# Joining the third product chain of a 512-token decoder's feed-forward units: one wide PSUM bank, read by a copy and additions

## The chip, the cores and the metric

The kernel runs on one core of a Trainium2 chip. Its time is the device time of one execution in microseconds (us); a lower time is better. The engines that matter here are TensorE (PE in the profile, with PEld for its weight loads), VectorE (DVE), ScalarE (ACT) and GpSimd (POOL, which here only issues transfers). Each takes its instructions in the order in which the program lists them, and waits at an instruction until what it needs is there. PSUM is the memory that TensorE writes its sums to; it is cut into banks of 512 float32 values for each of 128 partitions, and ScalarE and VectorE read it.

## The reference

A decoder trunk of two layers works on 512 tokens of 1024 channels. Each layer has a token mixer (a recurrent one in layer 0, a Conformer convolution in layer 1), a cross-attention into 256 memory tokens, and a gated feed-forward part. The change touches the feed-forward part alone:

```
def conv_ffn(x, norm, w_up, dw_w, dw_b, w_down):
    h = rms_norm(x, norm) @ w_up                      # 1024 -> 2 * 3072
    g = causal_dwconv(h[..., :D_FF], dw_w, dw_b)      # 3 taps along the tokens
    u = h[..., D_FF:]
    return (jax.nn.gelu(g) * u) @ w_down              # 3072 -> 1024
```

All numbers are float32. Products are made at more than one-pass precision: each operand is split into a high part (`hi`) and a low rest (`lo`), and `hi*hi + hi*lo + lo*hi` is summed.

## The kernel before, in words

The feed-forward part of a layer is worked in 24 *units*, one for each 128 hidden channels of the gate `g` and of the values `u`. Units 0 and 1 are plain; units 2 to 23 use a scheme of Strassen's kind with seven products of half size. A product multiplies one 512-by-128 block of weights (four chunks of 128 rows: `a11`, `a12`, `a22`, `s1` to `s4`) with one half-size operand made of the tokens (`T1` to `T4`, `B11`, `B21`, `B22`), for 256 tokens. Function `m` issues one product, by way of `Seven.product`. The sums of the products go to three *chains*, each a PSUM tile: `G` (products a11 and a12), `F` (a copy of a11, then s2, s3 and a22) and `H` (s1 and s4).

In a *narrow* product each chunk takes three matmuls over 256 columns (lines L187, L188, L189 of the helper `mm3`): `hi` weights on the high half of the operand, `hi` weights on its low half, `lo` weights on its high half. In a *joined* product the operand's high and low halves lie side by side, so that each chunk takes two matmuls (line L817): `hi` weights on all 512 columns, and `lo` weights on the first 256. The chain's bank then holds two halves that have to be added when it is read; `gather` does that with a ScalarE copy of the right half (L955) and a VectorE addition (L172, the line of the helper `add`). Units 6 to 21 (`WIDE`) have joined passes in `G` and `F`; `H` is narrow in all units. In these units `H` lies in the one bank of pool `stat` (`bufs=1`), so each unit takes the same bank again.

The order of every engine's work is written out by hand (`manual_schedule`). One unit `c`, in TensorE's order: s1 into `H`, s2 into `F`, a12 into `G`, s3 into `F`, 24 matmuls of the down projection into two `aux` banks, a11 of the next unit (`ahead`), s4 into `H`, a22 into `F`. `H` is read twice: after s3, for the right half of `f`, and at the unit's end, in `gating`, for the right half of `g`. `gating` is a generator: its first step stands at the end of its own unit, the others are woven into the next unit by `next(left, None)`.

Lines that the text speaks of, in a unit's order, beginning with the first step of `gating`: L172 addition of `H` to `g`; L961 `g` times the norm (VectorE); L939 first tap (ScalarE); L955 and L172 gather of `f`; L969 `f` times the norm; L942 two taps; L955 and L172 gather of `u` after s2; L899 two ScalarE copies that seed the `aux` banks; L944 GELU; L859 and L866 the high and low parts of a block of weights (ScalarE, then VectorE); L976 product of `f` and the gate; L979 and L981 its high and low parts; L201 and L204 the same of the down projection's weights; L904 two copies of the `aux` banks back to x; L992 the copy of the next unit's a11 chain into `F`.

Five lines that set the buffers:

```
    tmp = ctx.enter_context(tc.tile_pool(name="tmp", bufs=8))
    psum = ctx.enter_context(tc.tile_pool(name="ps", bufs=5, space=bass.MemoryType.PSUM))
    stat = ctx.enter_context(tc.tile_pool(name="stat", bufs=1, space=bass.MemoryType.PSUM))
    aux = ctx.enter_context(tc.tile_pool(name="aux", bufs=2, space=bass.MemoryType.PSUM))
    big = ctx.enter_context(tc.tile_pool(name="big", bufs=15))
```

Of the kernel before, what the change touches and what calls it, by code (L numbers as in the profile page):

```python
# [12 lines left out]
AF = mybir.ActivationFunctionType  # L13
# [8 lines left out]
M = 256  # L22
# [40 lines left out]
def trunk(ctx: ExitStack, tc: tile.TileContext, I: dict, out: list):  # L63
    nc = tc.nc
    V, A, G, PE = nc.vector, nc.scalar, nc.gpsimd, nc.tensor
# [14 lines left out]
    def nm(s):  # L80
        uid[0] += 1
        return f"{s}_{uid[0]}"

    def act_r():
        return act.tile([P, T], F32R, tag="act", name=nm("act"))
# [10 lines left out]
    def tmp_f(n=T):  # L96
        return tmp.tile([P, n], F32, tag="tmp", name=nm("tmp"))

    def main_ps():
        return psum.tile([P, T], F32, tag="mm", name=nm("mm"))  # L100
# [4 lines left out]
    wide = [True, 0]  # L105
# [6 lines left out]
    def stat_ps():  # L112
        return stat.tile([P, T], F32, tag="stat", name=nm("stat"))
# [57 lines left out]
    def add(out, a, b):  # L171
        V.tensor_tensor(out, a, b, op=ALU.add)  # L172
        return out
# [705 lines left out]
    def ffn(layer, norm, nxt, seven, pairs):  # L879
# [37 lines left out]
        def high(c, name):  # L917
            if c in pairs and (c, name) not in done:
                pairs[c].high(name)

        def low(c, name):
            if c in pairs and (c, name) not in done:
                pairs[c].low(name)
                done.add((c, name))

        def both(c, name):
            high(c, name)
            low(c, name)

        def times_r(out, ps, at):  # L930
            V.tensor_tensor(out[:, at], ps, norm.r[:, at], op=ALU.mult)

        left_half, right_half = slice(0, M), slice(M, T)

        def gate_conv(c, g):

            y = tmp_f()
            dw = lambda j: col("f_dw_w", (layer * 3 + j) * CF + c)
            A.activation(y, g, AF.Identity, scale=dw(2), bias=col("f_dw_b", layer * CF + c))  # L939
            yield y  # L940
            for s in (1, 2):
                V.scalar_tensor_tensor(y[:, s:], g[:, : T - s], dw(2 - s), y[:, s:], op0=ALU.mult, op1=ALU.add)  # L942
            yield y
            A.activation(y, y, AF.Gelu_apprx_tanh)  # L944
            yield y

        def wide(c):
            return c in WIDE
# [4 lines left out]
        def gather(out, ps):  # L953

            A.activation(out, ps[:, M:], AF.Copy)  # L955
            add(out, ps[:, :M], out)

        def gating(c, g, f, u, F, H):
            add(g[:, right_half], H, u[:, :M])
            if wide(c):  # L960
                V.tensor_tensor(g, g, norm.r, op=ALU.mult)  # L961
            else:
                V.tensor_tensor(g[:, right_half], g[:, right_half], norm.r[:, right_half], op=ALU.mult)
            conv = gate_conv(c, g)
            y = next(conv)
            yield
            if wide(c):
                gather(f[:, left_half], F)
                V.tensor_tensor(f, f, norm.r, op=ALU.mult)  # L969
            else:  # L970
                times_r(f, F, left_half)
            next(conv)
            yield
            next(conv)
            yield
            V.scalar_tensor_tensor(y, f, -1.0, y, op0=ALU.mult, op1=ALU.mult)  # L976
            yield
            ys[c] = act_r(), act_r()
            A.activation(ys[c][0], y, AF.Copy)  # L979
            yield  # L980
            V.tensor_tensor(ys[c][1], y, ys[c][0].bitcast(F32), op=ALU.subtract)  # L981

        def m(c, ps, block, j, first=True):
            seven.product(ps, pairs[c].w[block], j, first)

        def ahead(c):

            G, F = bank(c), bank(c)
            m(c, G, "a11", seven.B11)
            if c == WIDE[0] + 1:  # L990
                PE.matmul(F, pairs[c].w["a11"][0][:, :P], seven.both(seven.B11, 0), start=True, stop=True)
            A.activation(F, G, AF.Copy)  # L992
            return G, F

        def unit(c):

            nonlocal left, chains
            G, F = chains
            down, seeded = downs.get(c), c > GC
            H = (stat_ps if wide(c) else main_ps)()[:, :M]  # L1000
            m(c, H, "s1", seven.T1)
            if c <= second:
                high(c + 1, "s3")
            next(left, None)
            if c <= second:
                low(c + 1, "s3")

            m(c, F, "s2", seven.T2, False)
            u, f, g = tmp_f(), tmp_f(), tmp_f()
            if wide(c):  # L1010
                gather(u[:, :M], F)
            else:
                A.activation(u[:, :M], F, AF.Copy)
            if c == first:
                both(c + 2, "a11")
            if down:
                d = [down.bank(i, seeded) for i in range(2)]
            next(left, None)
            both(c + 1, "s3")
            next(left, None)  # L1020
            high(c + 1, "a22")

            m(c, G, "a12", seven.B21, False)
            next(left, None)
            next(left, None)
            high(c, "s4")
            if c == second:
                high(c + 2, "a11")
            low(c, "s4")
            if wide(c):  # L1030
                gather(g[:, left_half], G)
            elif c > second:
                times_r(g, G, left_half)

            m(c, F, "s3", seven.T3, False)
            if wide(c):
                gather(u[:, M:], F)
            else:
                A.activation(u[:, M:], F, AF.Copy)
            add(f[:, right_half], H, u[:, M:])  # L1040
            if c <= second:
                times_r(g, G, left_half)
            if c == second:
                low(c + 2, "a11")
            low(c + 1, "a22")
            if not wide(c):
                V.tensor_tensor(f[:, right_half], f[:, right_half], norm.r[:, right_half], op=ALU.mult)
            both(c + 2, "a11")
            high(c + 1, "a12")
            low(c + 1, "a12")  # L1050
            if c == WIDE[0] - 2:
                seven.put_aside()
            elif c == WIDE[0] - 1:
                seven.put_beside(seven.B21)
            if down:
                for ks in (range(GC - 1), (GC - 1,)):
                    for i in range(2):
                        down.products(i, d[i], seeded, ks)
            if c + 3 in pairs:
                pairs[c + 3].load()  # L1060
            if c + 2 in pairs and c > first:
                pairs[c + 2].load_second()
            if c > second and c + 1 in downs:
                downs[c + 1].w.high()
                downs[c + 1].w.low()
            if c + 2 in downs and first < c <= CF - 2:
                downs[c + 2].load()
            high(c + 1, "s1")
            low(c + 1, "s1")
            high(c + 1, "s2")  # L1070
            low(c + 1, "s2")
            if c == second:
                downs[c + 1].w.high()
                downs[c + 1].w.low()
            if down:
                down.home(0, d[0], seeded)

            if c + 1 in pairs:
                chains = ahead(c + 1)
            if down:  # L1080
                down.home(1, d[1], seeded)
            if c == WIDE[0] - 2:
                seven.put_beside(seven.B11)

            m(c, H, "s4", seven.B22, False)
            m(c, F, "a22", seven.T4, False)
            if c == WIDE[0] - 1:
                seven.put_beside(seven.B22)
            left = gating(c, g, f, u, F, H)
            next(left)  # L1090

# [87 lines left out]
        with tc.manual_schedule(engines=ORDERED):  # L1179
            opening()  # L1180
            for c in range(PLAIN, CF):
                unit(c)
            for _ in left:
                pass
# [801 lines left out]
```

## Time and profile before

| | before |
|---|---|
| time, median of 3 runs (lowest to highest) | 1423.07 us (1421.4 to 1423.74) |
| the profiled execution: its own time | 1425.19 us |
| the profiled execution: span of its trace | 1423.3 us |
| granted TensorE clock, mean | 0.998 |
| TensorE busy in the span | 1411.7 us |
| VectorE busy | 1115.4 us |
| ScalarE busy | 934.0 us |
| units 6 to 21 of layer 0 in the trace | 430.57 us to about 676 us |
| units 6 to 21 of layer 1 in the trace | 1114.81 us to about 1360 us |

The span is the stretch from the first to the last record of the trace. A row of the timeline has the start of a piece of work in us from the span's start, its length in us, the engine, the line, the operation, what it writes and reads, the shape, and how many instructions follow each other; in brackets stands the idle time before it and the instruction whose end it waited for. Two instructions of an engine that don't depend on each other overlap by their pipelines' length, so the next starts before the one before has ended.

### The profile page before, as it was taken

Reading aid. Unit: us, or ns where it says so; the run is one execution under the profiler, and the core shown is the slowest. Engines: PE = TensorE matmul, PEld = TensorE weight load, DVE = VectorE, ACT = ScalarE, POOL = GpSimd, SP = SyncE. Lnnn points to the kernel's source line nnn. Section 1 sums busy time; section 2 is a strip of 40 time slices with the busy share of each in tenths; the row PEclk is TensorE's granted clock in tenths of the full one; section 3 lists DMA queues with packets and bytes.
Section 4 is the critical chain, followed back from the end, with each engine's and each line's share of the span. In section 5 each row is a group of like instructions: output and inputs, shape, how many; then the busy total and the mean of one; then the engine's idle time right before and its main releaser. Section 6 shows DMA issues by size and latency. Waiting matters only on the chain.

```text
span 1423.3 us, 21777 instructions
## 1 busy us (share of the span) xinstructions
PE 1411.7 (99%) x8012; PEld 1228.0 (86%) x8012; DVE 1115.4 (78%) x1860; ACT 934.0 (66%) x1688; POOL 316.9 (22%) x333
## 2 busy tenths in 40 slices
PE   9999999999999999999999999999999999999998
PEld 7988888998898888888988777899889888888897
DVE  6987776778877777777789997968788777777775
ACT  7578744776577666666666547766756766666664
POOL 0001310110122222222008993011002222222211
PEclk9999999999999999999999999999999999999999
DMA  8523232544387777777433454345438777777741
GB/s 302 195 78 100 94 118 82 113 118 133 97 205 167 172 172 172 169 173 169 134 104 119 119 158 153 105 89 130 116 96 195 176 175 166 176 173 168 174 122 60
DMA packets 80027, 204.26 MB, mean 144 GB/s; under 512 B 9008, under 2 KB 9520, under 8 KB 79920
## 3 DMA queue, kind: packets, MB, share of 16 engines
q1 hardware_dynamic: 50832, 150.15, 32.4%
q0 software_dynamic: 28800, 52.44, 21.5%
q8 instruction: 63, 1.03, 0.3%
q14 instruction: 44, 0.36, 0.1%
q10 hardware_dynamic: 288, 0.27, 0.1%
HBM read 145.16 MB, written 2.10 MB: 103 GB/s over the span
## 4 chain that ended last, share of the span: by engine, by line
PE 86%; DVE 3%; issue 3%; DMA 3%; POOL 2%; ACT 2%; SPq 0%; POOLq 0%; ACTq 0%; DVEq 0%
PE mm L817 16%; PE mm L187 13%; PE mm L188 13%; PE mm L189 13%; PE aux L187 7%; PE aux L188 7%; PE aux L189 7%; PE stat L187 2%; PE stat L189 2%; PE stat L188 2%; PE mm L465 2%; DMA raw<-in_wv 1%; DVE wlo L168 1%; DMA raw<-wa 1%; ACT whi L167 1%
## 5 line engine op out<-in xcount | busy, mean ns | idle before, releaser
L187 PE MATMUL mm<-act,whi 128*128 128x512 f32 (+2 forms) x805 | 296.5, 370 | 0.9 <-ACT act L979 0.9
L188 PE MATMUL mm<-act,whi 128*128 128x512 f32 (+2 forms) x805 | 296.8, 369 | 0.6 <-DVE act L182 0.5
L189 PE MATMUL mm<-act,wlo 128*128 128x512 f32 (+2 forms) x805 | 296.5, 368 | 0.0
L187 PEld LDWEIGHTS mm<-act,whi 128*128 128x128 f32 x805 | 151.5, 188 | 27.2 <-ACT act L979 1.6
L188 PEld LDWEIGHTS mm<-act,whi 128*128 128x128 f32 x805 | 151.7, 188 | 26.5 <-DVE act L168 1.0
L189 PEld LDWEIGHTS mm<-act,wlo 128*128 128x128 f32 x805 | 151.7, 188 | 25.0 <-DVE wlo L168 0.6
L866 DVE TENSOR_TENSOR bigr<-raw,bigr 128x512 fp32r<-128x512 f32 x176 | 120.8, 687 | 61.0 <-ACT bigr L859 57.3
L187 PE MATMUL aux<-act,whi 128*128 128x512 f32 x399 | 155.6, 390 | 0.0
L188 PE MATMUL aux<-act,whi 128*128 128x512 f32 x399 | 155.5, 390 | 0.0
L189 PE MATMUL aux<-act,wlo 128*128 128x512 f32 x399 | 155.2, 389 | 0.0
L859 ACT ACTIVATE bigr<-raw 128x512 fp32r<-128x512 f32 x176 | 109.4, 623 | 69.8 <-DVE wlo L204 66.2
L872 POOL DMA_DIRECT2D raw<-wa x100 | 87.4, 893 | 299.7 <-DVE bigr L866 195.9
L167 ACT ACTIVATE whi<-raw 128x1024 fp32r<-128x1024 f32 (+1 forms) x95 | 96.4, 1020 | 86.6 <-PE mm L188 43.3
L817 PE MATMUL mm<-bigr,bigr 128*128 128x512 f32 (+1 forms) x768 | 150.6, 338 | 0.0
L817 PEld LDWEIGHTS mm<-bigr,bigr 128*128 128x128 f32 x768 | 118.3, 189 | 14.3
L869 POOL DMA_DIRECT2D raw<-raw x50 | 43.2, 865 | 371.7 <-DVE wlo L866 285.1
L172 DVE TENSOR_TENSOR tmp<-mm,tmp 128x256 f32<-128x256 f32 x194 | 77.8, 417 | 40.4 <-ACT tmp L955 37.9
L168 DVE TENSOR_TENSOR wlo<-raw,whi 128x1024 fp32r<-128x1024 f32 (+1 forms) x75 | 90.2, 1209 | 19.7 <-ACT whi L167 19.0
L817 PE MATMUL mm<-act,whi 128*128 128x512 f32 x256 | 95.5, 396 | 0.0
L189 PEld LDWEIGHTS aux<-act,wlo 128*128 128x128 f32 x399 | 74.9, 188 | 15.9
L188 PEld LDWEIGHTS aux<-act,whi 128*128 128x128 f32 x399 | 75.0, 188 | 15.5
L187 PEld LDWEIGHTS aux<-act,whi 128*128 128x128 f32 x399 | 75.0, 188 | 14.3
(378 smaller groups left out, 3504.9 us busy)
## 6 DMA issues: line engine op xcount, KB each, us to landing
raw<-wa POOLq DMA_DIRECT2D x150, 256.0 KB, 3.4
wa<-in_wpair SPq DMA_DIRECT2D x88, 256.0 KB, 3.8
raw<-in_wpair SPq DMA_DIRECT2D x44, 512.0 KB, 3.7
big<-in_wdown SPq DMA_DIRECT2D x42, 512.0 KB, 4.6
raw<-raw POOLq DMA_DIRECT2D x50, 256.0 KB, 4.0
raw<-in_pw SPq DMA_DIRECT2D x24, 512.0 KB, 3.3
raw<-in_win SPq DMA_DIRECT2D x20, 512.0 KB, 3.3
raw<-in_wk SPq DMA_DIRECT2D x16, 512.0 KB, 3.3
```

Source lines behind the costliest of these rows:

```text
L167: A.activation(hi, src, AF.Copy)
L168: fetched[1] = (eng or V).tensor_tensor(lo, src, hi.bitcast(F32), op=ALU.subtract)
L172: V.tensor_tensor(out, a, b, op=ALU.add)
L187: PE.matmul(ps, wh, xh, start=first, stop=False, skip_group_check=onto)
L188: PE.matmul(ps, wh, xl, start=False, stop=False, skip_group_check=onto)
L189: return PE.matmul(ps, wl, xh, start=False, stop=last, skip_group_check=onto)
L465: PE.matmul(p, m[j], x, start=k == 0 and j == 0 and x is hi, stop=k == C - 1 and x is lo)
L817: PE.matmul(to, part, by, start=first and c == 0 and i == 0, stop=c == 3 and i == 1, skip_group_check=True)
L859: A.activation(self.w[name][0], self.block(name), AF.Copy)
L866: V.tensor_tensor(lo, self.block(name), hi.bitcast(F32), op=ALU.subtract)
L869: G.dma_start(self.r, self.z, accum_op=ALU.add)
L872: G.dma_start(block, self.a22, accum_op=ALU.add)
```

## The change

In units 6 to 21 the chain `H` is joined too. Its tile is now the whole bank of 512 columns, and s1 and s4 take the form of two matmuls for each chunk, as in `G` and `F`. The bank's two halves are read so: for `f`, by two VectorE additions straight from the bank, one after the other; for `g`, by a ScalarE copy of the right half into a new tile `low_part` of pool `tmp`, an addition of the left half, and an addition of `low_part`.

```
         def gating(c, g, f, u, F, H):
-            add(g[:, right_half], H, u[:, :M])
             if wide(c):
+                low_part = tmp_f(M)
+                A.activation(low_part, H[:, M:], AF.Copy)
+            add(g[:, right_half], H[:, :M], u[:, :M])
+            if wide(c):
+                add(g[:, right_half], low_part, g[:, right_half])
                 V.tensor_tensor(g, g, norm.r, op=ALU.mult)
...
         def unit(c):
...
-            H = (stat_ps if wide(c) else main_ps)()[:, :M]
+            H = stat_ps() if wide(c) else main_ps()[:, :M]
             m(c, H, "s1", seven.T1)
...
-            add(f[:, right_half], H, u[:, M:])
+            add(f[:, right_half], H[:, :M], u[:, M:])
+            if wide(c):
+                add(f[:, right_half], H[:, M:], f[:, right_half])
```

On TensorE each of the products s1 and s4 goes from 12 matmuls of 256 columns to 4 of 512 and 4 of 256, in the same place. On the other engines the order shows what follows, for unit 8 of layer 0 (all units from 6 to 21 are alike). The names are those of the program with a running number; the numbers differ between the two programs.

ScalarE at the unit's end, before: the high part of block s2 of the next unit (L859), the two copies of the down projection's banks to x with the copy of a11 between them, the first tap, and the gathers of `f` and `u`. `waits` names the engines or transfer queues that the instruction has to wait for.

```order
L859 ACTIVATE bigr_4840<-raw_4504 128x512 [waits DMASW2_49,DVE_49]
L904 ACTIVATE x<-aux_4752 128x512 [waits PE_49]
L992 ACTIVATE mm_4846<-mm_4845 128x512 [waits PE_49]
L904 ACTIVATE x<-aux_4754 128x512
L939 ACTIVATE tmp_4879<-tmp_4749,par 128x512 [waits DVE_49]
L955 ACTIVATE tmp_4748<-mm_4686 128x256 [waits PE_49]
L955 ACTIVATE tmp_4907<-mm_4846 128x256 [waits PE_49]
```

The same place after the change (line numbers behind the edit are higher by 4 or 6):

```order
L859 ACTIVATE bigr_4829<-raw_4501 128x512 [waits DMASW2_49,DVE_49]
L904 ACTIVATE x<-aux_4740 128x512 [waits PE_49]
L996 ACTIVATE mm_4835<-mm_4834 128x512 [waits PE_49]
L904 ACTIVATE x<-aux_4742 128x512
L961 ACTIVATE tmp_4862<-stat_4713 128x256 [waits PE_49]
L939 ACTIVATE tmp_4867<-tmp_4737,par 128x512 [waits DVE_49]
L955 ACTIVATE tmp_4736<-mm_4679 128x256 [waits PE_49]
```

The copy of the bank's right half (L961) is a new row, behind the second L904 and ahead of the first tap.

VectorE in the unit's middle, before: the gather of `g`, the gather of `u` after s3, the addition of `H` to `f`, and the low parts of three blocks and of the down projection's weights.

```order
L172 TENSOR_TENSOR tmp_4749<-mm_4685,tmp_4749 128x256 [waits Activation_49]
L172 TENSOR_TENSOR tmp_4747<-mm_4686,tmp_4747 128x256 [waits Activation_49]
L172 TENSOR_TENSOR tmp_4748<-stat_4721,tmp_4747 128x256 [waits DVE_49]
L866 TENSOR_TENSOR bigr_4763<-wa_4667,bigr_4763 128x512 [waits DMAHW5_49]
L866 TENSOR_TENSOR wlo_4795<-raw_4665,whi_4794 128x512 [waits DMAHW0_49,Activation_49]
```

And after:

```order
L172 TENSOR_TENSOR tmp_4737<-mm_4678,tmp_4737 128x256 [waits Activation_49]
L172 TENSOR_TENSOR tmp_4735<-mm_4679,tmp_4735 128x256 [waits Activation_49]
L172 TENSOR_TENSOR tmp_4736<-stat_4713,tmp_4735 128x256 [waits DVE_49]
L172 TENSOR_TENSOR tmp_4736<-stat_4713,tmp_4736 128x256 [waits DVE_49]
L866 TENSOR_TENSOR bigr_4751<-wa_4660,bigr_4751 128x512 [waits DMAHW5_49]
L866 TENSOR_TENSOR wlo_4784<-raw_4658,whi_4783 128x512 [waits DMAHW0_49,Activation_49]
```

One addition from the bank follows the other, and it reads what the first has written.

VectorE at the unit's end, before: the low parts of s1 and s2 of the next unit, the addition of `H` to `g`, the multiplication by the norm, and the gather of `f`.

```order
L866 TENSOR_TENSOR bigr_4837<-raw_4504,bigr_4837 128x512 [waits DMASW1_49,Activation_49]
L866 TENSOR_TENSOR bigr_4840<-raw_4504,bigr_4840 128x512 [waits DMASW2_49,Activation_49]
L172 TENSOR_TENSOR tmp_4749<-stat_4721,tmp_4747 128x256 [waits PE_49]
L961 TENSOR_TENSOR tmp_4749<-tmp_4749,r_3614 128x512 [waits DVE_49]
L172 TENSOR_TENSOR tmp_4748<-mm_4686,tmp_4748 128x256 [waits Activation_49]
L969 TENSOR_TENSOR tmp_4748<-tmp_4748,r_3614 128x512 [waits DVE_49]
```

And after:

```order
L866 TENSOR_TENSOR bigr_4826<-raw_4501,bigr_4826 128x512 [waits DMASW1_49,Activation_49]
L866 TENSOR_TENSOR bigr_4829<-raw_4501,bigr_4829 128x512 [waits DMASW2_49,Activation_49]
L172 TENSOR_TENSOR tmp_4737<-stat_4713,tmp_4735 128x256 [waits Activation_49]
L172 TENSOR_TENSOR tmp_4737<-tmp_4862,tmp_4737 128x256 [waits DVE_49]
L965 TENSOR_TENSOR tmp_4737<-tmp_4737,r_3614 128x512 [waits DVE_49]
L172 TENSOR_TENSOR tmp_4736<-mm_4679,tmp_4736 128x256 [waits Activation_49]
L973 TENSOR_TENSOR tmp_4736<-tmp_4736,r_3614 128x512 [waits DVE_49]
```

The first addition from the bank, which waited for TensorE, now waits for ScalarE; a second addition, of the copied half, stands between it and the multiplication.

## The prediction

> **What bounds the kernel now.** I read the busy shares first, then one wide unit of layer 0 by stretches, then the timeline of that unit engine by engine, and last the table of waits over all wide units of the layer.
>
> ```profile
> PE 1411.7 (99%) x8012; PEld 1228.0 (86%) x8012; DVE 1115.4 (78%) x1860; ACT 934.0 (66%) x1688; POOL 316.9 (22%) x333
> 507.59:522.95 15.36, 15.36 (x90) 13.53 (x89) 11.80 (x20) 10.39 (x21) 3.45 (x5) 1.00 0.72 173
> ACT bigr L859 <- DVE wlo L204: 27.8, 15, 1.9
> 506.17 1.58 PE L817 MATMUL mm<-bigr,bigr 128*128 128x512 f32 x8
> 507.59 0.28 PE L187 MATMUL stat<-bigr,bigr 128*128 128x256 f32 x1
> 509.02 1.56 PE L817 MATMUL mm<-bigr,bigr 128*128 128x512 f32 x8
> 510.43 0.40 PE L817 MATMUL mm<-act,whi 128*128 128x512 f32 x1
> 511.83 1.58 PE L817 MATMUL mm<-bigr,bigr 128*128 128x512 f32 x8
> 520.11 0.28 PE L187 MATMUL stat<-act,bigr 128*128 128x256 f32 x1
> 521.53 0.75 PE L817 MATMUL mm<-bigr,bigr 128*128 128x512 f32 x3
> ```
>
> TensorE is the bound: in the unit from one s1 (507.59) to the next (522.95) it is busy for all of 15.36 us at full granted clock (1.00). VectorE works 11.80 us of that and ScalarE 10.39 us, so both look as if they had room. The question is where their idle time lies, and for that their rows stand here in time order, over a unit and into the next.
>
> ```profile
> 506.42 0.42 DVE L172 TENSOR_TENSOR tmp<-stat,tmp 128x256 f32<-128x256 f32 x1
> 506.87 0.69 DVE L961 TENSOR_TENSOR tmp<-tmp,r 128x512 f32<-128x512 f32 x1
> 508.71 0.42 DVE L172 TENSOR_TENSOR tmp<-mm,tmp 128x256 f32<-128x256 f32 x1 [1.15 <-ACT tmp L955]
> 509.17 0.69 DVE L969 TENSOR_TENSOR tmp<-tmp,r 128x512 f32<-128x512 f32 x1
> 509.78 1.53 DVE L942 SCALAR_TENSOR_TENSOR tmp<-tmp,par,tmp 128x511 f32<-128x511 f32 x2
> 511.23 0.42 DVE L172 TENSOR_TENSOR tmp<-mm,tmp 128x256 f32<-128x256 f32 x1
> 513.12 0.69 DVE L866 TENSOR_TENSOR bigr<-raw,bigr 128x512 fp32r<-128x512 f32 x1 [1.47 <-ACT bigr L859]
> 513.73 0.69 DVE L976 SCALAR_TENSOR_TENSOR tmp<-tmp,tmp 128x512 f32<-128x512 f32 x1
> 515.11 0.69 DVE L981 TENSOR_TENSOR act<-tmp,act 128x512 fp32r<-128x512 f32 x1 [0.70 <-ACT act L979]
> ...
> 517.10 0.42 DVE L172 TENSOR_TENSOR tmp<-stat,tmp 128x256 f32<-128x256 f32 x1
> 517.44 0.68 DVE L866 TENSOR_TENSOR bigr<-wa,bigr 128x512 fp32r<-128x512 f32 x1
> ...
> 519.24 1.22 DVE L204 TENSOR_TENSOR wlo<-big,whi 128x1024 fp32r<-128x1024 f32 x1
> 520.38 1.47 DVE L866 TENSOR_TENSOR bigr<-raw,bigr 128x512 fp32r<-128x512 f32 x2
> 521.77 0.42 DVE L172 TENSOR_TENSOR tmp<-stat,tmp 128x256 f32<-128x256 f32 x1
> 522.22 0.69 DVE L961 TENSOR_TENSOR tmp<-tmp,r 128x512 f32<-128x512 f32 x1
> ```
>
> ```profile
> 507.60 0.82 ACT L939 ACTIVATE tmp<-tmp,par 128x512 f32<-128x512 f32 x1 [0.33 <-DVE tmp L961]
> 508.32 0.36 ACT L955 ACTIVATE tmp<-mm 128x256 f32<-128x256 f32 x1
> 510.63 0.38 ACT L955 ACTIVATE tmp<-mm 128x256 f32<-128x256 f32 x1 [1.95 <-PE mm L817]
> 511.95 0.62 ACT L944 ACTIVATE tmp<-tmp 128x512 f32<-128x512 f32 x1
> 512.47 0.62 ACT L859 ACTIVATE bigr<-raw 128x512 fp32r<-128x512 f32 x1
> 514.45 0.63 ACT L979 ACTIVATE act<-tmp 128x512 fp32r<-128x512 f32 x1 [0.84 <-DVE tmp L976]
> 520.49 0.63 ACT L859 ACTIVATE bigr<-raw 128x512 fp32r<-128x512 f32 x1 [1.85 <-DVE wlo L204]
> 521.03 0.58 ACT L904 ACTIVATE x<-aux 128x512 f32<-128x512 f32 x1
> 521.51 0.59 ACT L992 ACTIVATE mm<-mm 128x512 f32<-128x512 f32 x1
> 522.03 0.59 ACT L904 ACTIVATE x<-aux 128x512 f32<-128x512 f32 x1
> ```
>
> These idle times are not room: VectorE and ScalarE hand work to each other all around the unit. From L961 at 506.87, each step starts within 0.05 us of the end of its input, or as soon as its engine takes the next instruction: L961, L939, gather of `f` (L955, L172), L969, L942; L944, L859, L866 (513.12), L976, L979, L981, low parts up to L204; its end (519.24 + 1.22 = 520.46) lets ScalarE make the high part of s2 (520.49; the table shows the same wait in 15 units), whose low part is the second L866 of the row at 520.38, and then L172 (521.77) and L961 again (522.22). This **loop** of two engines takes 522.22 - 506.87 = 15.35 us, like TensorE, with one slack: L942 ends at 509.78 + 1.53 = 511.31, but L944 starts only at 511.95 (its engine waited 1.95 us for TensorE ahead of it). So the loop's own length is 15.35 - (511.95 - 511.34) = 14.74 us, 0.61 us below the period.
>
> **The change part by part.** *TensorE.* A joined product takes 1.40 to 1.42 us from its start to that of the next (506.17 to 507.59, 509.02 to 510.43, 510.43 to 511.83), a narrow one 1.43 (507.59 to 509.02) and 1.42 (520.11 to 521.53). Against a joined mean of 1.41 that saves 0.02 and 0.01 us; bounds are 0 and 0.05. In 32 wide units it is 1.0 us, with TensorE alone at 15.33 us a unit. No weight load or transfer is added, and SP's and POOL's issues keep their places.
>
> *Second addition for `f`.* Behind 517.10 stands a dependent addition. A dependent step after such an addition comes 0.45 us later (506.42 to 506.87), an independent one 0.34 (517.10 to 517.44); here the second addition waits for the first, then L866 follows it at 0.34, so the step after is later by 0.45. All steps from L866 to L204 and to ScalarE's 520.49 move with it: **+0.45 us** in the loop.
>
> *Copy of `H`'s right half.* It stands behind the second L904, and the first addition to `g` now waits for ScalarE, not for TensorE. The trace has no such copy; the nearest row is the gather's copy of the same shape from PSUM, 0.36 to 0.38 us, and I take 0.37. From ScalarE's 520.49: L904 +0.54, L992 +0.48, L904 +0.52, the copy +0.48 (the step from 521.03 to 521.51), its length 0.37, hand-over 0.03: 2.42 us to the addition. Before, it started 521.77 - 520.49 = 1.28 us after. That is **+1.14 us**. Bounds: 1.10 with a copy of 0.36 and no hand-over, and 1.35 if the copy took the 0.58 us of a copy of double width (521.03).
>
> *Second addition for `g`.* It reads SBUF; a row of two SBUF operands of this shape has the same 0.42:
>
> ```profile
> L764 DVE TENSOR_TENSOR tmp<-tmp,tmp 128x256 f32<-128x256 f32 x16 | 6.7, 419 | 0.7 <-ACT tmp L758 0.7
> ```
>
> It depends on the first addition, and L961 on it: **+0.45 us** (bound below: 0.34, the step of an independent one).
>
> *The new loop* is 14.74 + 0.45 + 1.14 + 0.45 = 16.78 us, over TensorE's 15.33. Each period grows by 16.78 - 15.35 = 1.43 us, and TensorE waits at two places. First at s1: the single `stat` bank is free only when the first addition to `g` has ended (before, 521.77 + 0.42 = 522.19, 0.76 us ahead of 522.95). Second at s3, which writes `F` and must wait for the gather of `u` to have read it (before, 511.23 + 0.42 = 511.65 against 511.83: 0.18 us of slack). After the change that addition stands behind L942, which ends later: from the bank's release, L961 is at +0.48, L939 +1.21, L955 +1.93, L172 +2.32, L969 +2.78, L942 +3.39, the gather of `u` +4.84 to +5.26, all by the steps above. For TensorE to resume after a wait I take 0.16 us, an estimate between nothing and the 0.28 us of the matmul at 507.59; it is the same at s1 and s3, so s3 stands 5.26 us behind s1, where the products need 1.41 + 1.40 + 1.40 = 4.21: 1.05 us of the wait falls at s3, and about 0.43 at s1.
>
> *Edges.* In the first wide unit only the addition for `f` and the end are new. Its rows:
>
> ```profile
> 443.49 0.63 ACT L859 ACTIVATE bigr<-raw 128x512 fp32r<-128x512 f32 x1 [1.85 <-DVE wlo L204]
> 446.15 0.28 PE L187 MATMUL stat<-bigr,bigr 128*128 128x256 f32 x1
> ```
>
> 443.49 + 0.45 + 2.42 + 0.42 + 0.16 = 446.94, so the next s1 is 0.79 us later. Fourteen periods follow (unit 7's s1 to unit 21's): 14 x 1.43 = 20.02. Unit 21 still waits at s3 (1.05, less about 0.06 for joined products): +0.99; unit 22 has `H` in another pool, and its gather of `u` has no addition, so the chain there runs out in idle time. A layer loses 0.79 + 20.02 + 0.99 = 21.8 us, two layers 43.6.
>
> *Covers.* The fifth `tmp` tile of a unit costs nothing as I read the order: the copy waits for TensorE alone. The accumulating transfers behind L866 move with VectorE, and what reads them moves as well.
>
> *A rule.* Could the copy and the first addition read the bank's halves side by side? The order says no, by the wait for ScalarE. The Trainium skill, "PSUM — Partial Sum Buffer", section "PSUM bank collisions raise a hardware error", says that a ScalarE read and a VectorE read of one bank at once are a collision even at disjoint columns, and have to be kept apart by a semaphore. By that the sum stays; without it the first rival below would hold. No row of before shows two such reads at once.
>
> **The rivals.** *The two reads overlap.* If the new wait is for an older ScalarE instruction, the first addition is done beside the copy, and the loop loses 0.45: 16.33 us, +0.98 a unit. The first edge is about 0.35, so (0.35 + 14 x 0.98 + 0.99) x 2 = 30.1, or 1453 us. For it: two halves hold different data. Against it: an older instruction would already have been waited for by the L866 just ahead, which takes ScalarE's high part.
>
> *Hidden, no change.* VectorE gains 0.84 us and ScalarE 0.37 in a unit where they idle 3.56 and 4.97. It decides if what is added to the loop stays under 15.33 - 14.74 = 0.59 us, as it would if ScalarE's 1.85 us wait were for a transfer and not for L204, so that the loop were open there. Then TensorE's saving is left: 1422 us. Against it: the wait ends with L204 each time, and the addition for `f` alone uses up 0.45.
>
> *The loops feed each other.* TensorE's waits could delay a gather that ScalarE then waits for, and a late transfer could add to it. At 0.3 us a unit this gives 1467 + 10 = 1477 us. Against: after s3 the next reader on ScalarE (the gather of `u`) stands behind the high part of s4, over 1 us after the product's end.
>
> **How the numbers follow.** The longer loop gets 0.80, overlapping reads 0.09, hidden 0.06, feeding loops 0.05. The profiled execution took 1425.19 us on a span of 1423.3; its span would become 1466.9 and its time 1468.8. It stands 2.1 us above the median of the runs, which the same growth brings to 1423.07 + 43.6 = 1466.7 us; that is the forecast. An error of 0.15 us in the loop moves it by 30 x 0.15 = 5; the range takes that in and reaches down to overlapping reads: 1452 to 1475. Within 0.2% (2.8 us, about what a measurement can tell) lies the hidden case alone, 0.05; 0.01 is left for a gain and 0.94 for a loss.
>
> **What would show it.** Right: wide units 16.6 to 16.9 us long, TensorE waiting for VectorE (L172) at s1 and s3, VectorE's and ScalarE's busy time up by 27 and 12 us, units outside 6 to 21 as before. Wrong: unit length near 15.35 with no TensorE waits; or 16.3 with the addition beside the copy; or waits of L859 for transfers, which I hold to be covered.

## The result, and the profile after

The kernel after takes 1471.31 us (median of 4 runs, 1470.34 to 1472.55) against 1422.4 us before (4 runs, 1421.4 to 1423.74): a ratio of 1.0344, with a 95% interval of 1.0331 to 1.0357, or 47 to 51 us more. The forecast was 1466.7 us, in a range of 1452 to 1475. The two traces differ by less, 1469.6 - 1423.3 = 46.3 us, because the execution of before that was profiled (1425.19 us) lay 2.8 us above the median of its runs.

First the busy times and the shares of the chain that ended last, from the page of the kernel after:

```profile
PE 1426.5 (97%) x7756; PEld 1214.6 (83%) x7756; DVE 1145.4 (78%) x1924; ACT 945.3 (64%) x1720; POOL 316.9 (22%) x333
PE 55%; DVE 22%; ACT 13%; issue 5%; DMA 2%; POOL 2%; SPq 0%; DVEq 0%; ACTq 0%; POOLq 0%
```

And a wide unit of layer 0 of the same kernel, from one s1 to the next, in the view by stretches (the stretch and its length; busy time, and count in brackets, of PE, PEld, DVE, ACT and POOL; granted clock, transfer share, GB/s):

```profile
514.31:531.21 16.90, 15.85 (x81) 13.07 (x81) 12.74 (x23) 10.74 (x21) 3.15 (x4) 1.00 0.65 157
```

The unit has gone from 15.36 to 16.90 us, and its 16.90 us repeat to 0.01 us from the second interval of a layer to the last. Before, TensorE made up 86% of the chain that ended last; now it is 55%, and VectorE and ScalarE have 35% between them. The clock is full, so TensorE isn't slow; it waits. Where it waits stands in TensorE's timeline, with s4, a22, the next unit's s1, s2, a12 and s3:

```profile
511.05 1.58 PE L817 MATMUL stat<-act,bigr 128*128 128x512 f32 x8
512.47 1.57 PE L817 MATMUL mm<-bigr,bigr 128*128 128x512 f32 x8
514.31 1.68 PE L817 MATMUL stat<-bigr,bigr 128*128 128x512 f32 x8 [0.28 <-DVE tmp L172]
515.83 1.56 PE L817 MATMUL mm<-bigr,bigr 128*128 128x512 f32 x8
517.23 0.39 PE L817 MATMUL mm<-act,whi 128*128 128x512 f32 x1
519.58 1.68 PE L817 MATMUL mm<-bigr,bigr 128*128 128x512 f32 x8 [0.78 <-DVE tmp L172]
```

The table of TensorE's waits over the whole run of the kernel after (time in total, times, longest, in us):

```profile
PE mm L817 <- DVE tmp L172: 23.5, 30, 0.8
PE stat L817 <- DVE tmp L172: 8.8, 30, 0.6
```

Both waits are for additions (L172) of VectorE: at s1 for the bank, at s3 for the gather of `u`. VectorE and ScalarE, in the order of the rows shown of before, look like this (L961 on ScalarE is the new copy, L965 and L973 are the old L961 and L969, L980 the old L976):

```profile
513.83 0.42 DVE L172 TENSOR_TENSOR tmp<-stat,tmp 128x256 f32<-128x256 f32 x1 [1.06 <-ACT tmp L961]
514.29 0.42 DVE L172 TENSOR_TENSOR tmp<-tmp,tmp 128x256 f32<-128x256 f32 x1
514.75 0.69 DVE L965 TENSOR_TENSOR tmp<-tmp,r 128x512 f32<-128x512 f32 x1
517.66 1.53 DVE L942 SCALAR_TENSOR_TENSOR tmp<-tmp,par,tmp 128x511 f32<-128x511 f32 x2
519.11 0.42 DVE L172 TENSOR_TENSOR tmp<-mm,tmp 128x256 f32<-128x256 f32 x1
521.08 0.69 DVE L980 SCALAR_TENSOR_TENSOR tmp<-tmp,tmp 128x512 f32<-128x512 f32 x1
524.46 0.88 DVE L172 TENSOR_TENSOR tmp<-stat,tmp 128x256 f32<-128x256 f32 x2
525.26 0.68 DVE L866 TENSOR_TENSOR bigr<-wa,bigr 128x512 fp32r<-128x512 f32 x1
...
527.06 1.22 DVE L204 TENSOR_TENSOR wlo<-big,whi 128x1024 fp32r<-128x1024 f32 x1
530.73 0.42 DVE L172 TENSOR_TENSOR tmp<-stat,tmp 128x256 f32<-128x256 f32 x1 [1.06 <-ACT tmp L961]
```

```profile
515.48 0.82 ACT L939 ACTIVATE tmp<-tmp,par 128x512 f32<-128x512 f32 x1 [1.68 <-DVE tmp L965]
519.28 0.63 ACT L944 ACTIVATE tmp<-tmp 128x512 f32<-128x512 f32 x1 [0.46 <-DVE tmp L942]
519.82 0.62 ACT L859 ACTIVATE bigr<-raw 128x512 fp32r<-128x512 f32 x1
528.31 0.63 ACT L859 ACTIVATE bigr<-raw 128x512 fp32r<-128x512 f32 x1 [2.31 <-DVE wlo L204]
...
529.84 0.59 ACT L904 ACTIVATE x<-aux 128x512 f32<-128x512 f32 x1
530.32 0.38 ACT L961 ACTIVATE tmp<-stat 128x256 f32<-128x256 f32 x1
```

The GELU (L944) used to wait for TensorE's part of ScalarE's queue; now it waits for L942, so the last slack in the loop of the two engines is gone, and nowhere in it is a step that waits for TensorE. It closes after 16.90 us: the first addition to `g` starts at 513.83 and again at 530.73. The three additions to the loop can be read off: 524.46 to 525.26 for two additions where one took 0.34 us (+0.46); 528.31 to 530.73, 2.42 us where it was 1.28 (+1.14); 513.83 to 514.29 for the second addition to `g` (+0.46).

### The profile page after: what moved, and what is told of

Its sections match the earlier page's. It is cut to its first block, busy times and chain, and to the rows that moved or that the text cites. A ratio compares the mean times of both kernels' runs of the same rounds, so it can differ in the third digit from the quotient of the medians.

```text
span 1469.6 us, 21331 instructions
## 1 busy us (share of the span) xinstructions
PE 1426.5 (97%) x7756; PEld 1214.6 (83%) x7756; DVE 1145.4 (78%) x1924; ACT 945.3 (64%) x1720; POOL 316.9 (22%) x333
## 4 chain that ended last, share of the span: by engine, by line
PE 55%; DVE 22%; ACT 13%; issue 5%; DMA 2%; POOL 2%; SPq 0%; DVEq 0%; ACTq 0%; POOLq 0%
PE mm L187 14%; PE mm L188 14%; PE mm L189 14%; DVE tmp L172 5%; DVE bigr L866 3%; PE aux L188 3%; PE aux L187 3%; PE aux L189 3%; DVE tmp L942 3%; DVE wlo L204 2%; ACT bigr L859 2%; ACT x L904 2%; DVE wlo L866 2%; ACT tmp L939 2%; DVE tmp L965 1%
## 5 line engine op out<-in xcount | busy, mean ns | idle before, releaser
L817 PE MATMUL mm<-bigr,bigr 128*128 128x512 f32 (+1 forms) x768 | 153.8, 343 | 23.5 <-DVE tmp L172 23.5
L859 ACT ACTIVATE bigr<-raw 128x512 fp32r<-128x512 f32 x176 | 109.3, 622 | 83.5 <-DVE wlo L204 81.0
L817 PEld LDWEIGHTS mm<-bigr,bigr 128*128 128x128 f32 x768 | 122.0, 188 | 49.2 <-DVE tmp L172 33.1
L172 DVE TENSOR_TENSOR tmp<-mm,tmp 128x256 f32<-128x256 f32 x194 | 77.9, 418 | 38.9 <-ACT tmp L955 37.8
```

The lines of the kernel that those rows point to most:

```text
L817: PE.matmul(to, part, by, start=first and c == 0 and i == 0, stop=c == 3 and i == 1, skip_group_check=True)
L859: A.activation(self.w[name][0], self.block(name), AF.Copy)
```

## The experiments

Four explanations were set against each other. *Loop*: a unit lasts as long as the longest ring of work that hands on from engine to engine, and the change lengthened the ring of VectorE and ScalarE. *Bank*: what counts is how long the single `stat` bank is held after s4. *Form*: joined matmuls are slow in that bank. *Busy time*: each added instruction costs its length. The length of a unit is that between the starts of s1. The first interval of a layer's wide stretch is left out, and in two runs the second (16.28 us in the detour without joined matmuls, 16.47 with s3 first); the others of a run agree to about 0.03 us either way, and where they spread more, the range is given.

**The joined matmuls alone.**

```
-            if wide(c):
-                low_part = tmp_f(M)
-                A.activation(low_part, H[:, M:], AF.Copy)
             add(g[:, right_half], H[:, :M], u[:, :M])
             if wide(c):
-                add(g[:, right_half], low_part, g[:, right_half])
...
-            if wide(c):
-                add(f[:, right_half], H[:, M:], f[:, right_half])
```

> H is joined on TensorE, but only its left half is read, as before: the right half (the products with the operand's low part) is left out of f and g, and with it the copy and both second additions. Loop theory (the wide unit's length is the larger of TensorE's 15.33 us and the loop of VectorE and ScalarE, which this leaves at about 14.84): 1421 to 1423 us, a wide unit 15.30 to 15.35 us, no TensorE waits. Rival, that the joined form in the stat bank itself is slow there: most of the 48.9 us stays, 1460 to 1471.

Measured: 1422.56 us against 1422.36, ratio 0.9999 (0.9989 to 1.0008); a unit 15.31 to 15.36 us, as the loop theory had it. *Form* falls: the whole loss is in the reading of the second half.

**With the second addition for `f`.** The edit is as above, with the last two lines kept.

> As the run with the matmuls alone, with the second addition for f put back; g still lacks the right half. Loop theory: 14.84 + 0.46 = 15.30 us, just under TensorE's 15.33, so 1421 to 1424 us although VectorE has 32 additions more. A theory that each added VectorE instruction costs its own length: 1422 + 32 x 0.46 = 1437.

Measured: 1429.24 us, ratio 1.0044 (1.0029 to 1.0059); a unit 15.56 us. A miss for both: half of the addition's 0.46 us shows. The loop at 15.30 us should have stayed under TensorE. What it ran into is a ring over two units. TensorE's wait at s3 (for the gather of `u`, behind L942) makes the next s2 late, the next gather of `u` and so the GELU wait for that, and the delay runs on over L204 and `H` into the gather of the unit after. Two periods of it hold the new addition once, so a unit grows by half. It is read off the order of the waits in the trace; no run changed it alone. These are its rows in one unit, in the order of their starts:

```profile
510.75 1.53 DVE L942 SCALAR_TENSOR_TENSOR tmp<-tmp,par,tmp 128x511 f32<-128x511 f32 x2
511.32 0.39 ACT L955 ACTIVATE tmp<-mm 128x256 f32<-128x256 f32 x1 [1.67 <-PE mm L817]
512.20 0.42 DVE L172 TENSOR_TENSOR tmp<-mm,tmp 128x256 f32<-128x256 f32 x1
512.64 0.62 ACT L944 ACTIVATE tmp<-tmp 128x512 f32<-128x512 f32 x1
512.67 1.68 PE L817 MATMUL mm<-bigr,bigr 128*128 128x512 f32 x8
```

The GELU (512.64) starts 0.36 us after L942 has ended (512.28): what holds it is ScalarE's queue behind the copy that waited for s2. And s3 (512.67) starts as soon as the gather's addition behind L942 has ended (512.62).

**The second addition for `g` from the bank, without the copy.**

```
-            if wide(c):
-                low_part = tmp_f(M)
-                A.activation(low_part, H[:, M:], AF.Copy)
...
-                add(g[:, right_half], low_part, g[:, right_half])
+                add(g[:, right_half], H[:, M:], g[:, right_half])
```

> The whole result, without the ScalarE copy: the second addition for g reads the bank itself, as that for f does. Loop theory: 14.84 + 0.46 + 0.46 = 15.76 us a wide unit, about +0.41 on before, so 1422 + 28 x 0.41 + 1 = 1435 (1431 to 1439), with the wait at s3 and none or little at s1. Rival, that the hold on the single stat bank after s4 is what counts: the bank comes free 0.45 us later than before, where 0.76 us was to spare, so 1421 to 1423.

Measured: 1436.47 us, ratio 1.0095 (1.0080 to 1.0110); a unit 15.73 to 15.92 us, 15.79 in the mean, inside the loop theory's range. The copy and the detour over ScalarE's queue are worth 35 of the 49 us, although ScalarE has the time.

**A step of the loop taken out, far from the bank.**

```
             if wide(c):
                 gather(f[:, left_half], F)
-                V.tensor_tensor(f, f, norm.r, op=ALU.mult)
```

> The kernel after, with the multiplication of f by the norm (VectorE, in the next unit's first third) left out of the wide units, so f is unscaled there; nothing between s4 and the release of the bank changes. Loop theory: the loop is shorter by that step, 0.61 us, so 16.29 us a unit and 1471 - 30 x 0.61 = 1453 (1450 to 1456). Bank rival: the path from s4 over the copy and the addition to the next s1 is as long as it was, so 1468 to 1472.

Measured: 1454.4 us, ratio 1.0223 (1.0207 to 1.0238); a unit 16.36 us, inside the loop theory's range. *Bank* alone can't explain that; taking 0.6 us from a step that isn't between s4 and the bank's release gave 17 us back. The unit is 0.07 us longer than the loop's 16.29, which a later run explains.

**The detour without joined matmuls**, in the kernel before:

```
+            if wide(c):
+                low_part = tmp_f(M)
+                A.activation(low_part, H, AF.Copy)
+                H = low_part
             add(g[:, right_half], H, u[:, :M])
```

> The kernel before, with narrow H and the same matmuls, but g takes H by way of a ScalarE copy at the unit's end and one addition of the copy; no addition more. Nothing is left out. Loop theory: 14.84 + 1.14 = 15.98 us a unit, +0.63, so 1422 + 30 x 0.63 = 1441 (1437 to 1445), without any joined matmul. Bank rival: the bank is free when the copy ends, near when it was needed before, so 1422 to 1426.

Measured: 1444.09 us, ratio 1.0146 (1.0131 to 1.0162); a unit 15.95 to 16.02 us. The detour costs its 1.14 us less the slack (14.74 + 1.14 = 15.88, and about 0.1 us in hand-overs, as in the kernel after), whatever the matmuls' form, and the number of VectorE instructions is that of before (1860). *Busy time* falls with it: ScalarE worked 945.5 us where it worked 934.0, 11.5 us more, and the run took 21.3 us longer.

**ScalarE's order: the high part of s3 ahead of the GELU.** The kernel after, with this edit in `unit`:

```
-            next(left, None)
-            both(c + 1, "s3")
+            if wide(c):
+                high(c + 1, "s3")
+                next(left, None)
+                low(c + 1, "s3")
+            else:
+                next(left, None)
+                both(c + 1, "s3")
```

> The kernel after, with ScalarE's high part of block s3 moved ahead of the GELU in wide units (before it stood behind). VectorE's low part of s3 then no longer waits for the GELU and the copy behind it. Nothing is left out. Loop theory: the loop is shorter by about 1.0 us (0.63 us between L866 and the GELU's user, and the rest of the copy's 0.62), so 15.9 us a unit and 1471 - 30 x 1.0 = 1441 (1436 to 1447). Bank rival: nothing near the bank moves, 1468 to 1472.

Measured: 1448.81 us, ratio 1.0183 (1.0169 to 1.0197); a unit 16.16 us. The direction is right, 22.5 us come back, but 30 were expected. With it and the addition from the bank together:

> Both: the second addition for g reads the bank itself, and the high part of s3 stands ahead of the GELU. Nothing is left out. Loop theory: 15.76 - 1.0 = 14.76 us, under TensorE's 15.33, so all of the loss goes and TensorE's 1 us is gained: 1420.5 to 1422.5. If the two steps don't add up, a unit stays over 15.4 us: 1425 to 1435.

Measured: 1435.4 us, ratio 1.0089 (1.0075 to 1.0103); a unit 15.74 us: hardly better than the addition from the bank alone (1436.47), and 0.4 us outside the wider of the two ranges, so the sum failed. The trace of this run shows what holds it; s3, and the first addition to `g` of that unit:

```profile
507.27 0.88 DVE L172 TENSOR_TENSOR tmp<-stat,tmp 128x256 f32<-128x256 f32 x2 [0.37 <-PE stat L817]
512.55 0.42 DVE L172 TENSOR_TENSOR tmp<-mm,tmp 128x256 f32<-128x256 f32 x1
513.02 1.68 PE L817 MATMUL mm<-bigr,bigr 128*128 128x512 f32 x8 [0.16 <-DVE tmp L172]
523.02 0.88 DVE L172 TENSOR_TENSOR tmp<-stat,tmp 128x256 f32<-128x256 f32 x2 [0.35 <-PE stat L817]
```

VectorE now waits for TensorE's s4, and TensorE for VectorE's gather of `u`. That is a **second ring**: s3 to the end of s4 and the addition, 513.02 to 523.02, 10.0 us; from there to the next s3, 507.27 to 513.02, 5.75 us; together the 15.75 of the unit. With the copy and its hand-over in between (0.38 + 0.03 us) it is the 16.16 us of the run before. In the kernel before the same ring is about 5.2 + 10.0 us, an estimate from the rows of its unit, a shade under TensorE's 15.33.

The control, the same move in the kernel before:

> The kernel before, with only the high part of s3 moved ahead of the GELU. Loop theory: TensorE bounds before, so nothing changes, 1421.5 to 1423. A theory that the move is good by itself: faster by 5 us or more.

Measured: 1423.0 us against 1422.83, ratio 1.0001 (0.9992 to 1.0010), a unit 15.35 us.

**The copy that gathers `f` ahead of the first tap.** It shortens both rings: the gather's addition and the multiplication of `f` by the norm run while ScalarE makes the tap. The edit, here on the kernel after alone:

```
+            if wide(c):
+                A.activation(f[:, left_half], F[:, M:], AF.Copy)
             conv = gate_conv(c, g)
             y = next(conv)
             yield
             if wide(c):
-                gather(f[:, left_half], F)
+                add(f[:, left_half], F[:, :M], f[:, left_half])
```

> The kernel after with the second move alone: the copy that gathers f ahead of the first tap. Loop theory: 16.90 - 1.23 = 15.67 us for the loop of VectorE and ScalarE, which binds again, so 1422 + 30 x 0.33 = 1432 (1428 to 1437). Bank rival: nothing between s4 and the bank's release moves, 1468 to 1472.

Measured: 1453.94 us, ratio 1.0211 (1.0197 to 1.0225); a unit 16.37 us. Both theories miss. And with the other move:

> The kernel after with all its work (copy, both second additions, single stat bank), and two moves in ScalarE's order in wide units: the high part of s3 ahead of the GELU, and the copy that gathers f ahead of the first tap. The runs so far show, beside the loop of VectorE and ScalarE (16.90 us in the kernel after), a second one through TensorE: s3, ..., s4, reading of H, ..., gather of u, next s3 (16.16 us in the kernel after, seen where the first loop was shortened). The second move takes 1.2 us out of both, the first 0.85 out of the first alone: 14.8 and 14.9 us, both under TensorE's 15.33. Loop theory: 1421 to 1425 us, a unit of 15.31 to 15.4 us. Theories that the loss is the added work's busy time, the copy as such, or the single bank: 1445 to 1471.

Measured: 1438.78 us, ratio 1.0103 (1.0089 to 1.0116); a unit 15.84 us. Two thirds of the loss come back with all the work in place, but not all: again a miss for both. The trace of this run, in the order of the ring:

```profile
509.71 0.42 DVE L172 TENSOR_TENSOR tmp<-stat,tmp 128x256 f32<-128x256 f32 x1 [1.07 <-ACT tmp L961]
510.19 1.66 PE L817 MATMUL stat<-bigr,bigr 128*128 128x512 f32 x8 [0.26 <-DVE tmp L172]
513.29 0.39 ACT L955 ACTIVATE tmp<-mm 128x256 f32<-128x256 f32 x1 [1.11 <-PE mm L817]
514.62 0.62 ACT L859 ACTIVATE bigr<-raw 128x512 fp32r<-128x512 f32 x1
515.27 0.69 DVE L866 TENSOR_TENSOR bigr<-raw,bigr 128x512 fp32r<-128x512 f32 x1 [1.10 <-ACT bigr L859]
...
521.86 1.22 DVE L204 TENSOR_TENSOR wlo<-big,whi 128x1024 fp32r<-128x1024 f32 x1
```

This is a **third ring**, and it runs through the single bank: the first addition to `g` frees the bank, s1 starts (0.26 us of wait), s2 follows, the gather of `u` waits for it (1.11), the high part of s3 and all of VectorE's work to L204 (its end at 523.08) follow, and behind L204 the high part of s2, the two L904 with the copy of a11 between them, and the copy of `H` lead back to the addition, 509.71 + 15.84 = 525.55. So the bank theory was right in part. In the kernel after, whose order is the same behind the gather of `u`, this ring is the 16.37 us of the run with the gather moved alone; it is also what the run without the norm's step came to rest on (16.36; its GELU starts 0.28 us after L942 has ended, so its first ring has slack there). At 16.90 us the first ring covers it.

**Both moves, and the second addition for `g` from the bank.**

> The same two moves, with the second addition for g reading the bank itself in place of the copy. Loop theory: both loops below TensorE's 15.33 us, 1421 to 1423.5. If a third loop that spans two units binds, as it did with the addition for f alone (15.56 us): 1426 to 1430.

Measured: 1422.98 us against 1423.14, ratio 0.9997 (0.9988 to 1.0005). All of the loss is gone, with joined matmuls, four additions that read the bank in each unit, and no copy of it. And the control, narrow `H` with the two moves:

> The kernel before with the same two moves, narrow H. Loop theory: TensorE bounds, nothing changes: 1421.5 to 1423.5. Against it, if the moves are worth something by themselves: under 1419. The difference of this run and the one before is what joined products in H are worth once nothing waits: 0 to 1.5 us.

Measured: 1423.34 us, ratio 0.9996 (0.9987 to 1.0005). In the same unit of the two runs, the joined one first, VectorE works 0.77 us more, and the unit is as long (the view by stretches, first of the kernel with joined matmuls and both additions from the bank):

```profile
506.87:522.20 15.33, 15.33 (x81) 13.11 (x80) 12.75 (x23) 10.40 (x20) 3.44 (x5) 1.00 0.71 173
```

and the same view of the control with narrow `H`:

```profile
507.47:522.81 15.34, 15.34 (x90) 13.50 (x88) 11.98 (x20) 10.40 (x20) 3.45 (x4) 1.00 0.72 173
```

| kernel | unit, us | what holds it |
|---|---|---|
| before; matmuls alone; controls | 15.33 to 15.36 | TensorE |
| second addition for `f` alone | 15.56 | ring over two units (read from the trace) |
| both additions from the bank | 15.79 | first ring (15.76 by the sum), the second beside it (15.74) |
| detour without joined matmuls | 15.99 | first ring |
| after | 16.90 | first ring |
| after, s3 first | 16.16 | second ring |
| after, gather first; after without a step | 16.37; 16.36 | third ring |
| after, both moves | 15.84 | third ring |
| both additions from the bank, both moves | 15.33 | TensorE |

No version beats the kernel before by more than a measurement can tell.

## Why the prediction was right, and where its sum was off

*The bound and the ring.* Right. That the loop of VectorE and ScalarE at 14.74 us is what the change would break was the step on which all else hung; the run with a step removed, the detour alone and the return to 15.33 us by two moves and a direct addition show it.

*The three prices.* +0.45, +1.14 and +0.45 us were forecast, 0.46, 1.14 and 0.46 measured. The copy took 0.38 us against 0.37.

*The period.* This is the mis-sized term: growth of 1.43 us a unit was forecast, and it was 16.90 - 15.35 = 1.55. Of the missing 0.12 us, 0.06 lies in the slack ahead of the GELU: a hand-over of 0.03 us from L942 was assumed, and 519.28 - (517.66 + 1.53) = 0.09 measured. 0.02 more lies in L859 behind it, which follows at 0.54 us where it followed at 0.52, 0.02 in the two dependent additions; the rest is in hundredths. Over 28 periods that is 3.4 us.

*The waits.* 1.05 us at s3 and 0.43 at s1 were forecast. Measured against joined products of 1.41 us, s3 starts 519.58 - 517.23 - 1.41 = 0.94 us late and takes 0.10 longer (its first weight load starts only with it, at 519.58), s1 starts 514.31 - 512.47 - 1.41 = 0.43 late and takes as much longer. The prediction's two waits add up to 1.48 us, where its own period leaves 16.78 - 15.33 = 1.45; the forecast of the time doesn't hang on that.

*The edges.* The first interval grew by 0.66 us, where 0.79 was forecast. The end of the wide stretch and the program behind it grew by 0.4 us in layer 0, where 0.99 was forecast, and by 1.2 in layer 1. In layer 0 part of what was lost came back at the end of the feed-forward part, where TensorE had waited 0.9 us for ScalarE's high part of the gated product (L979, now L983) and now waits 0.2.

*The total.* 43.6 us were forecast; the traces differ by 46.3 and the medians by 48.9. The step between the last two is the profiled execution of before, 2.8 us over the median; where in that execution the 2.8 us lie was not traced. The forecast of 1466.7 us also stood on 1423.07 us, the median of three runs of before, where four now give 1422.4. So of the 4.6 us by which it fell short, 2.7 are the sum's own (3.4 too little for the period, 0.7 too much for the rest), and 1.9 come from the profiled executions and medians that the sum was set on; these are not explained.

*The other signs.* The wait of L859 ended with L204, as forecast, and the first s1 of layer 0 comes as before (430.44 against 430.57 us). ScalarE's busy time rose by 11.3 us, where 12 were forecast, VectorE's by 30.0, where 27 were: 64 additions of 0.42 us are 26.9, and the first addition to `g`, which now waits, no longer overlaps the low part ahead of it by 0.08 us (before, 520.38 + 1.47 = 521.85 against 521.77), which makes 2.6 us in 32 units.

*TensorE's gain.* Forecast at 1 us with nothing waiting, with a bound of nothing; the runs show nothing, as below. It could not change the result, since TensorE was no longer the bound.

*The rivals.* Overlapping reads: no, the addition starts 0.03 us after the copy's end (530.32 + 0.38 = 530.70 to 530.73). The Trainium skill ("PSUM — Partial Sum Buffer", section "PSUM bank collisions raise a hardware error") asks for that order, and the trace agrees in that no read by ScalarE and read by VectorE of the bank overlap in it; what happens if they do, no run here shows. Hidden: no, the run is 49 us longer. Loops that feed each other: not in the kernel after, where the rings of 16.37 and 16.16 us lie under 16.90, but they decided six of the experiments, and five of the twelve forecasts made for the experiments missed because of them. The prediction knew only the first ring and compared it with TensorE's time alone; that no other ring was longer in the kernel after was luck.

## What to carry to other kernels

Idle time of an engine isn't room for work: two engines that are busy for 77% and 68% of a unit and hand work to each other form a ring whose length, not their busy time, is to be compared with the bound. Before adding a step, find every ring through the place where it goes, also those through the bound engine and a single buffer, and write their lengths side by side; the next one caps what a repair gives back. Here two moves in ScalarE's order gave 32.5 of 49 us back with every instruction in place.

## What the hardware showed that was not expected

Joining `H` does not make TensorE faster, though each joined product is shorter than the narrow one it replaces. These are s1, s2, a12, s3 and the first matmul of the down projection, joined throughout (first fence), and with a narrow s1 (second fence):

```profile
522.20 1.58 PE L817 MATMUL stat<-bigr,bigr 128*128 128x512 f32 x8
523.62 1.58 PE L817 MATMUL mm<-bigr,bigr 128*128 128x512 f32 x8
525.03 0.40 PE L817 MATMUL mm<-act,whi 128*128 128x512 f32 x1
526.45 1.58 PE L817 MATMUL mm<-bigr,bigr 128*128 128x512 f32 x8
527.86 0.40 PE L187 MATMUL aux<-act,whi 128*128 128x512 f32 x1
```

```profile
522.81 0.28 PE L187 MATMUL stat<-bigr,bigr 128*128 128x256 f32 x1
524.25 1.56 PE L817 MATMUL mm<-bigr,bigr 128*128 128x512 f32 x8
525.65 0.40 PE L817 MATMUL mm<-act,whi 128*128 128x512 f32 x1
527.05 1.56 PE L817 MATMUL mm<-bigr,bigr 128*128 128x512 f32 x8
528.45 0.39 PE L187 MATMUL aux<-act,whi 128*128 128x512 f32 x1
```

The joined s1 takes 1.42 us where the narrow one takes 1.44, but the three joined products behind it take 1.41, 1.42 and 1.41 in place of 1.40 each, so that the four take 5.66 us against 5.64. The joined s4 gains 0.01 us (1.41 against 1.43), so that the whole unit is the same within 0.01 us. Why a row of joined products runs 0.01 us slower each when it doesn't begin behind a narrow one stays open.
